# A list scheduler for the expert phase of a hybrid decoder layer on one Trainium2 core: 512-column weight pieces of half the rows, and evictions on either of two engines

## The chip, the cores and the metric

The kernel runs on 1 core of one Trainium2 chip. The metric is the device time of one execution in microseconds (us). Before the change it is 2073.69 us, the median of 3 runs (2073.25 to 2075.34).

The engines are named as in the profile: PE multiplies matrices (PEld is its loading of weights, which overlaps PE), ACT applies functions element by element, DVE combines tensors element by element, POOL issues the indirect transfers (gathers and scatters through a list of rows), and SP issues the plain transfers. Each engine works through its own queue in the order in which the program was written, and an instruction that waits holds back all that stand behind it.

## The reference, cut to what matters

The layer works on 1024 tokens of 1024 features in float32. Its first part (norm, gated linear attention and a state-space model, output projection, router) is the same in both kernels. The change lies in the second part, a mixture of experts: each token goes to 4 of 32 experts.

```
logits = xt @ router_w + router_b;  top_val, top_idx = top_k(logits, 4);  gate = softmax(top_val)
for each expert e, for the tokens that chose it (x: [n, 1024]):
    gu = x @ w_gu[e] + b_gu[e]                  # w_gu[e]: [1024, 2048]: g is the first half, up the second
    g, up = min(g, 7), clip(up, -7, 7)
    act = (up + 1) * (g * sigmoid(1.702 * g))
    y = act @ w_down[e] + b_down[e]             # w_down[e]: [1024, 1024]
    out[token] += gate * y
```

So 32 x 12 = 384 pieces of 1024 x 1024 bytes of weights are read once (402.7 MB as the profile counts).

## The kernel before, in words

**Tokens and experts.** The router writes a list of tokens for each expert, and the experts are ranked by falling count. Each rank has a fixed capacity `CAPS[r]` (396, 272, 260 ... 36; 4,648 in all; this is the column count C of its products). `GROUPS` puts the ranks into 8 groups of four with about 580 columns each, the last being ranks 3, 26, 5 and 31 (252, 68, 228, 36 columns). A group has a gate-up phase (all four experts, `w_gu`) and a down phase (all four, `w_down`).

**Weights.** A chunk is 1024 x 1024 bytes: 256 columns of all 1024 rows, so 384 chunks. SP loads it into one of 6 staging slots (`ST`, L1592). `split_chunk` makes two fp16 parts out of it, in one of 7 places (`WH`, `WL`): ACT writes the high part (L1596), and DVE, which needs ACT's result, the low part (L1597). The staging slot is free for the next load only when DVE is done.

**Products.** `products` takes one column tile of 128 at a time: for each of 8 row tiles one product of the high weights with the high tokens (L1618), one with the low tokens (L1619), one of the low weights with the high tokens (L1620). A chunk is 2 x 8 x 3 = 48 products of C columns.

**Evictions.** `run_unit` returns what is left to do with a unit's result, and the main loop puts it ahead of the next unit: ACT evicts the gate (L1661) and the up part (L1664), DVE clips and multiplies (L144, L147), ACT and DVE make the two fp16 parts (L159, L147). In the down phase ACT evicts the result (L1683) into a ring that holds 792 columns. `moe_out` then takes a block of up to 128 tokens and half of the features: 4 transposes on PE (L1697), an eviction scaled by the gate on ACT (L159, tile `A<-ax,S`) into one of 3 buffers `yt`, and a scatter with addition on POOL (L1699) into `ff_d[0]` or `ff_d[1]` in DRAM. A scatter waits for the one before it on the same half, and a `yt` buffer is free when its scatter has landed. There are 51 blocks, so 102 scatters.

**Tokens of the next group.** During a down phase POOL gathers the next group's tokens (L1602), PE transposes them (L1610, 8 for each block), and ACT (L159, tile `S<-tr`) and DVE (L147) make fp16 parts.

**What sets the order.** The order of every queue is that of the calls in the main loop. `split_to` puts splits as far ahead as the 7 places allow, `put_out` puts an output block after about 2 us of products.

## Time and profile before

| | |
|---|---|
| time, median of 3 runs | 2073.69 us |
| span of the profiled execution (first to last instruction) | 2069.1 us |
| first part, up to the first weight load of the experts | 588 us |
| expert phase, up to the last scatter's landing | about 1441 us |
| final norm and residual | about 39 us |
| PE / DVE / ACT busy, share of the span | 88% / 71% / 63% |
| moved by DMA | 540.83 MB, mean 261 GB/s |

The profiled execution's own time is shown only as its span; the median of the runs is 4.6 us more than that, which is what lies around the span. "Busy" of PE counts matmuls with modelled ends, so the idle time beside it is a lower bound. The granted clock is that of PE, 1.00 being the upper of its two levels (2.4 GHz). A DMA share over 1 means that transfers overlapped on an engine.

### The profile page before, as it was taken

The page shows a single profiled execution, that of the slowest core. Times are in us where ns is not written, and L with a number is a line of the kernel's source. Part 1 is how long each engine was busy: PE and PEld are TensorE (multiplying, and loading weights), DVE is VectorE, ACT ScalarE, POOL GpSimd, SP SyncE. Part 2 cuts the span into 40 slices and gives each one's busy share as a digit, 9 for nine tenths or more (in the row PEclk, how much of TensorE's full clock was granted, in tenths as well). Part 3 has the DMA queues.
Part 4 walks back from the last instruction along what each step waited for, and adds up shares of the span by engine and source line. Part 5 has one row for each costly group of instructions (what it writes and reads, how often), then busy time and mean ns, then how long its engine had stood idle before and what let it go on. Part 6 is the DMA issues. An engine that isn't in the chain of part 4 may idle for free. (4 is left out here: it accounts for less than half of the span.)

```text
span 2069.1 us, 53438 instructions
## 1 busy us (share of the span) xinstructions
PE 1831.0 (88%) x22354; PEld 1634.6 (79%) x22354; DVE 1465.9 (71%) x2361; ACT 1294.2 (63%) x1997; POOL 473.8 (23%) x495
## 2 busy tenths in 40 slices
PE   7678899999978999998998998999699899999950
PEld 3566788787868998997987998766599789999950
DVE  5766536567748976985894897686589668878825
ACT  3524133643326877886885887776688677888831
POOL 4720112204531033024013303201320230140033
PEclk9999899999979999999999999999899999999985
DMA  9076554323379999999999999999799999999964
GB/s 310 31 206 123 157 173 147 128 83 123 112 211 307 335 336 304 348 329 291 343 346 267 322 349 327 310 325 315 221 320 349 284 286 334 338 331 342 345 177 170
DMA packets 493413, 540.83 MB, mean 261 GB/s; under 512 B 41234, under 2 KB 459248, under 8 KB 493136
## 3 DMA queue, kind: packets, MB, share of 16 engines
q1 hardware_dynamic: 456112, 469.51, 72.4%
q0 software_dynamic: 30384, 60.49, 11.7%
q10 hardware_dynamic: 6672, 7.38, 1.1%
q8 instruction: 177, 2.90, 0.6%
q14 instruction: 68, 0.56, 0.1%
HBM read 489.57 MB, written 45.61 MB: 259 GB/s over the span
## 5 line engine op out<-in xcount | busy, mean ns | idle before, releaser
L1597 DVE SCALAR_TENSOR_TENSOR E<-A,E 128x2048 f16<-128x2048 f32 x110 | 250.5, 2289 | 92.1 <-ACT E L1596 89.4
L1699 POOL DMA_INDIRECT ff_d<-A,S x102 | 205.9, 2019 | 464.4 <-ACT A L159 252.4
L1597 DVE SCALAR_TENSOR_TENSOR B<-A,B 128x2048 f16<-128x2048 f32 x110 | 250.7, 2290 | 73.8 <-ACT B L1596 73.4
L1597 DVE SCALAR_TENSOR_TENSOR C<-A,C 128x2048 f16<-128x2048 f32 x110 | 250.5, 2289 | 52.0 <-ACT C L1596 48.8
L1620 PE MATMUL mm<-S,B 128*128 128x148 f16 (+27 forms) x1328 | 260.1, 234 | 2.9 <-DVE B L1597 2.4
L1618 PE MATMUL mm<-S,B 128*128 128x148 f16 (+27 forms) x1328 | 260.0, 234 | 2.8 <-ACT B L1596 2.1
L1618 PE MATMUL mm<-S,E 128*128 128x164 f16 (+27 forms) x1344 | 253.1, 231 | 10.2 <-ACT S L1683 10.2
L1619 PE MATMUL mm<-S,B 128*128 128x148 f16 (+27 forms) x1328 | 259.8, 233 | 0.6 <-issue 0.4
L1620 PE MATMUL mm<-S,E 128*128 128x164 f16 (+27 forms) x1344 | 253.2, 230 | 1.5 <-issue 1.5
L1619 PE MATMUL mm<-S,E 128*128 128x164 f16 (+27 forms) x1344 | 253.0, 230 | 0.9 <-issue 0.9
L1618 PE MATMUL mm<-S,C 128*128 128x92 f16 (+25 forms) x1296 | 241.2, 230 | 3.8 <-ACT S L1683 3.8
L1620 PE MATMUL mm<-S,C 128*128 128x92 f16 (+25 forms) x1296 | 241.0, 229 | 0.0
L1619 PE MATMUL mm<-S,C 128*128 128x92 f16 (+25 forms) x1296 | 240.9, 229 | 0.0
L1602 POOL DMA_INDIRECT S<-hn_d,S x51 | 80.5, 1578 | 687.6 <-PE tr L1610 647.8
L1596 ACT ACTIVATE B<-A 128x2048 f16<-128x2048 f32 x110 | 209.9, 1924 | 31.7 <-DMA A<-in_exp_w_gu_dram 27.7
L1596 ACT ACTIVATE E<-A 128x2048 f16<-128x2048 f32 x110 | 210.1, 1923 | 17.7 <-DMA A<-in_exp_w_gu_dram 9.0
L1596 ACT ACTIVATE C<-A 128x2048 f16<-128x2048 f32 x110 | 209.9, 1924 | 16.9 <-DMA A<-in_exp_w_gu_dram 9.6
L1619 PEld LDWEIGHTS <-E 128*128 128x128 f16 x1760 | 167.7, 99 | 18.8 <-issue 11.3
L1619 PEld LDWEIGHTS <-C 128*128 128x128 f16 x1760 | 171.6, 100 | 11.0 <-issue 4.3
L159 ACT ACTIVATE A<-ax,S 128x512 f32<-128x512 f32 (+17 forms) x102 | 68.5, 685 | 178.1 <-DMA ff_d<-A,S 154.2
L1618 PEld LDWEIGHTS <-B 128*128 128x128 f16 x1760 | 170.7, 99 | 10.7 <-ACT B L1596 2.4
L1619 PEld LDWEIGHTS <-B 128*128 128x128 f16 x1760 | 171.3, 100 | 9.7 <-issue 3.1
(345 smaller groups left out, 5130.0 us busy)
## 6 DMA issues: line engine op xcount, KB each, us to landing
A<-in_exp_w_gu_dram SPq DMA_DIRECT2D x256, 1024.0 KB
A<-in_exp_w_down_dram SPq DMA_DIRECT2D x128, 1024.0 KB
S<-in_ada_w_dram POOLq DMA_DIRECT2D x64, 256.0 KB, 3.1
S<-in_ada_w_dram SPq DMA_DIRECT2D x16, 512.0 KB
S<-in_w_in_dram SPq DMA_DIRECT2D x8, 1024.0 KB
S<-in_x_dram SPq DMA_DIRECT2D x12, 512.0 KB
ff_d<-S POOLq DMA_DIRECT2D x18, 256.0 KB, 6.1
S<-in_w_out_dram SPq DMA_DIRECT2D x8, 512.0 KB
```

Source lines behind the costliest of these rows:

```text
L159: A.activation(o, i, AF.Copy, scale=scale)
L1596: i_ = A.activation(wh, st, AF.Copy, scale=WS)
L1597: i_ = V.scalar_tensor_tensor(wl, st, WS, wh, op0=OP.mult, op1=OP.subtract, accum_out=acc_col())
L1602: P.indirect_dma_start(out=x_[0:cb], out_offset=None, in_=hn2_d, in_offset=bass.IndirectOffsetOnAxis(ap=x.lt[0:cb, b, 0:1], axis=0))
L1618: i_ = PE.matmul(o, wh[:, k, cols], mh[:, k], start=(k == 0), stop=False)
L1619: PE.matmul(o, wh[:, k, cols], ml[:, k], start=False, stop=False)
L1620: i_ = PE.matmul(o, wl[:, k, cols], mh[:, k], start=False, stop=(k == 7))
L1699: P.indirect_dma_start(out=ff_d[h], out_offset=bass.IndirectOffsetOnAxis(ap=lt[0:cb, b, 0:1], axis=0), in_=yt[0:cb], in_offset=None, compu ...
```

## The change

Pieces of weights are now 512 columns of half the rows (4 row tiles): still the same size and 384 of them, with rows of 2 KB in place of 1 KB. A unit (`sub_jobs`) is the gate, the up part or the result for up to 4 column tiles (2 where C is over 256). It works one piece after the other: first the 32 products with the piece's high part, then the 16 with its low part; the second piece's products add to the first's. The evictions of the up part, of its high fp16 part, of the down results, of the tokens' high part and of the output blocks may go to ACT or to DVE (`scaled`). The places for the gate are two of 1024 columns, for the up part one.

Every step is a `Job` with the engines it may run on, a duration, a due place, and the jobs it comes after. `run_jobs` walks through them at build time with a clock of its own for each engine, and at each step puts out the job that can start first (the earlier due place first on a tie); so it settles the order of all five queues and the engine of each eviction. The groups, the order of experts, the number of staging slots, of fp16 places, of `yt` buffers and of banks stay as they are. The two tables for tokens beyond the capacities (`overflow_table`) move from the fourth to the seventh unit to ahead of the first.

```diff
-    ST = [carve(t_, 0, 8, 256) for t_ in SA[:-1]]
+    ST = [carve(t_, 0, 4, 512) for t_ in SA[:-1]]
     WT.append(SA[-1])
     WH, WL = [], []
     for t_ in WT:
-        WH.append(carve(t_, 0, 8, 128).bitcast(F16))
-        WL.append(carve(t_, 4, 8, 128).bitcast(F16))
+        WH.append(carve(t_, 0, 4, 256).bitcast(F16))
+        WL.append(carve(t_, 4, 4, 256).bitcast(F16))
...
+    gs_r, u_t = [carve(e2, 0, 1024), carve(e2, 4, 1024)], carve(e3, 0, 1024)
...
-    def split_chunk(n):
-        st, wh, wl = ST[n % NST], WH[n % NWS], WL[n % NWS]
-        i_ = A.activation(wh, st, AF.Copy, scale=WS)
-        i_ = V.scalar_tensor_tensor(wl, st, WS, wh, op0=OP.mult, op1=OP.subtract, accum_out=acc_col())
...
+            x, name, col, kh = chunks[n]
+            load_expert(x)
+            SP.dma_start(ST[n % NST], I[name][0][ds(x.e, 1), 512 * kh:512 * kh + 512, col:col + 512]
+                         .rearrange("o (k p) c -> p (o k) c", p=128))
+    def split_hi(n):
+        A.activation(WH[n % NWS], ST[n % NST], AF.Copy, scale=WS)
+    def split_lo(n):
+        V.scalar_tensor_tensor(WL[n % NWS], ST[n % NST], WS, WH[n % NWS], op0=OP.mult, op1=OP.subtract,
+                               accum_out=acc_col())
...
+    def scaled(e, o, i, scale, bias=None):
+        if e == "ACT":
+            A.activation(o, i, AF.Copy if bias is None else AF.Identity, scale=scale,
+                         **({} if bias is None else {"bias": bias}))
+        elif bias is None:
+            ts(o, i, scale, OP.mult)
+        else:
+            ts(o, i, scale, OP.mult, bias, OP.add)
...
+    class Job:
+        def __init__(self, on, due, after, put, lag=0.0, behind=None):
+            self.on, self.due, self.put, self.lag = on, due, put, lag
+            self.after, self.behind = [j for j in [behind] + after if j is not None], behind
+            self.end, self.at = None, None
+            jobs.append(self)
+    def act_us(n, psum=False, parts=1):
+        return parts * (0.30 if psum else 0.22) + n / 1200
+    def dve_us(n, parts=1, rate=960):
+        return 0.13 * parts + n / rate
+    def run_jobs():
+        free = {e: 0.0 for e in ("PE", "ACT", "DVE", "POOL", "SP")}
+        users, left = {}, {}
+        for j in jobs:
+            left[id(j)] = len(j.after)
+            for a_ in j.after:
+                users.setdefault(id(a_), []).append(j)
+        open_ = [j for j in jobs if not j.after]
+        def ready(j, e):
+            return max([0.0] + [a_.end - (a_.lag if a_ is j.behind else -0.2 * (a_.at != e)) for a_ in j.after])
+        while open_:
+            best = None
+            for e in free:
+                mine = [(max(ready(j, e), free[e]), j.due, n, j) for n, j in enumerate(open_) if e in j.on]
+                if not mine:
+                    continue
+                first_ = min(m[0] for m in mine)
+                t_, due, n, j = min((m for m in mine if m[0] <= first_ + 1e-9), key=lambda m: (m[1], m[2]))
+                if best is None or (t_, due) < best[:2]:
+                    best = (t_, due, e, j)
+            t_, _, e, j = best
+            open_.remove(j)
+            j.at, free[e] = e, t_ + j.on[e]
+            j.end = free[e] + j.lag
+            j.put(e)
+            for u in users.get(id(j), ()):
+                left[id(u)] -= 1
+                if not left[id(u)]:
+                    open_.append(u)
+        assert all(j.end is not None for j in jobs)
+        return max(free.values())
...
+    subs, phase = [], []
+    for gi, g in enumerate(GROUPS):
+        phase.append((len(chunks), len(subs)))
+        for c in range(2):
+            for r in g:
+                for q, kind in enumerate("gu"):
+                    subs += [(kind, ex[r], c, js, len(chunks)) for js in (J4 if CAPS[r] <= 256 else J2)]
+                    chunks += [(ex[r], "exp_w_gu", 1024 * q + 512 * c, kh) for kh in range(2)]
+        phase.append((len(chunks), len(subs)))
+        for r in g:
+            for c in range(2):
+                subs += [("d", ex[r], c, js, len(chunks)) for js in (J4 if CAPS[r] <= 256 else J2)]
+                chunks += [(ex[r], "exp_w_down", 512 * c, kh) for kh in range(2)]
+    last_use, first_use = {}, {}
+    for i, u in enumerate(subs):
...
+        ld[n] = Job({"SP": 2.95}, n, [hi_.get(n - NST), lo_.get(n - NST)], put, lag=2.0, behind=ld.get(n - 1))
+        if n < len(chunks):
+            due = first_use[n]
+            hi_[n] = Job({"ACT": act_us(2048)}, due - 0.5, [ld[n], use.get(n - NWS), hi_.get(n - 1)], lambda e: split_hi(n))
+            lo_[n] = Job({"DVE": dve_us(2048) + 0.1}, due, [hi_[n], lo_.get(n - 1)], lambda e: split_lo(n))
...
+            t_ = Job({"PE": 0.46}, due, [gat, tr_free[q]], transpose)
+            h_ = Job({"ACT": act_us(4 * cb, True), "DVE": dve_us(4 * cb)}, due, [t_] + after[1:],
+                     lambda e, pt=pt, o_=o_: scaled(e, x.xh[o_], pt[:, :, 0:cb], XS))
+            tr_free[q] = Job({"DVE": dve_us(4 * cb) + 0.1}, due, [h_], lows)
...
+        t_ = Job({"PE": 0.46}, due, after + [ot_free[q]], transpose)
+        ot_free[q] = Job({"ACT": act_us(512, True), "DVE": dve_us(512)}, due + 2, [t_, yt_free[y]],
+                         lambda e: scaled(e, yt[0:cb], pt[0:cb].rearrange("p a b -> p (a b)"),
+                                          x.lt[0:cb, b, 1:2].bitcast(F32)))
+        yt_free[y] = added[c] = Job({"POOL": 1.7}, due, [ot_free[q], added[c]],
+                                    lambda e: P.indirect_dma_start(
+                                        out=ff_d[c], out_offset=bass.IndirectOffsetOnAxis(ap=x.lt[0:cb, b, 0:1], axis=0),
+                                        in_=yt[0:cb], in_offset=None, compute_op=OP.add), lag=7.0)
...
+        def highs(kh):
+            def put(e):
+                wh = WH[(n + kh) % NWS]
+                for q, j in enumerate(js):
+                    for k in range(4):
+                        w_, f_ = wh[:, k, 128 * j:128 * j + 128], 4 * kh + k
+                        PE.matmul(pp[q], w_, mh[:, f_], start=(f_ == 0 and q % per == 0), stop=False, skip_group_check=True)
+                        PE.matmul(pp[q], w_, ml[:, f_], start=False, stop=False, skip_group_check=True)
+            return put
+        def lows(kh):
+            def put(e):
+                wl = WL[(n + kh) % NWS]
+                for q, j in enumerate(js):
+                    for k in range(4):
+                        PE.matmul(pp[q], wl[:, k, 128 * j:128 * j + 128], mh[:, 4 * kh + k], start=False,
+                                  stop=(kh == 1 and k == 3), skip_group_check=True)
+            return put
+        for kh in range(2):
+            s_ = Job({"PE": 2 * us}, 2 * i + kh, [step[0], hi_[n + kh]] + (needs if kh == 0 else []), highs(kh))
+            step[0] = Job({"PE": us}, 2 * i + kh, [s_, lo_[n + kh]], lows(kh))
+            use[n + kh] = step[0]
+        due, end = 2 * i + 4, step[0]
...
+            ev = Job({"ACT": act_us(w, True, nj), "DVE": dve_us(w, nj)}, due, [end, u_free[0]], linear)
+            u_free[0] = Job({"DVE": dve_us(w, 2) + w / 1920}, due, [ev, gj], clamp)
+            ah = Job({"ACT": act_us(w), "DVE": dve_us(w, 1, 1920)}, due + 2, [u_free[0]],
+                     lambda e: scaled(e, x.ah[:, f0:f0 + nj], g3, XS))
+            gs_free[q] = Job({"DVE": dve_us(w)}, due + 2, [ah],
+                             lambda e: stt(x.al[:, f0:f0 + nj], g3, XS, x.ah[:, f0:f0 + nj], OP.mult, OP.subtract))
...
-    first_tokens(0)
     tables = [overflow_table(0, capr), overflow_table(1, None)]
...
+    for t_ in tables:
+        take(t_, 2)
...
+    run_jobs()
```

**DVE at the start.** The stretch begins with the copies of the transposed biases. Before (the first low part follows at once; S is the plain float32 area, tr a bank of transposes, A, B, C, E are slots of staging and fp16 parts):

```order
L1708 COPY E_4724<-tr 128x256
L142 TENSOR_SCALAR E_4724<-tr 128x256
L1708 COPY E_4724<-tr 128x256
L1597 SCALAR_TENSOR_TENSOR B_4573,A_4732<-A_4725,B_4573 128x2048
L147 SCALAR_TENSOR_TENSOR S,A_4732<-tr,S 128x4x128 x2
L147 SCALAR_TENSOR_TENSOR S,A_4732<-tr,S 128x4x76 x2
L1597 SCALAR_TENSOR_TENSOR B_4574,A_4732<-A_4726,B_4574 128x2048
```

Now, from the end of the second table on:

```order
L1498 TENSOR_REDUCE S<-S 128x1
L148 SCALAR_TENSOR_TENSOR S<-S 128x1
L1500 TENSOR_REDUCE S<-S 128x1
L133 TENSOR_TENSOR S<-S 128x1
L1507 COPY S<-tr 1x129
L1588 SCALAR_TENSOR_TENSOR B_4573,A_4732<-A_4725,B_4573 128x2048
L1588 SCALAR_TENSOR_TENSOR B_4574,A_4732<-A_4726,B_4574 128x2048
L148 SCALAR_TENSOR_TENSOR S,A_4732<-tr,S 128x4x128 x2
```

Both tables, 16 instructions and a copy each, now stand between the copies and the first low part (L1588), and two low parts stand ahead of the first tokens' low parts.

**ACT in a down phase.** This is where ranks 2 and 27 (260 and 60 columns) give their results; `A_4732<-ax,S` is the eviction of an output block into `yt`. Before:

```order
L1596 ACTIVATE C_4576<-A_4726 128x2048
L159 ACTIVATE A_4732<-ax,S 128x512 x2
L159 ACTIVATE A_4732<-ax,S 4x512
L1683 ACTIVATE S<-ax,E_4724 128x60 x2
L1596 ACTIVATE E_4577<-A_4727 128x2048
L159 ACTIVATE S<-tr 128x368 x2
L1683 ACTIVATE S<-mm,E_4724 128x60 x2
L1596 ACTIVATE E_4578<-A_4728 128x2048
```

Now:

```order
L1602 ACTIVATE A_4732<-ax,S 128x512
L1585 ACTIVATE C_4575<-A_4725 128x2048
L1602 ACTIVATE A_4732<-ax,S 4x512
L1585 ACTIVATE C_4576<-A_4726 128x2048
L1602 ACTIVATE S<-mm,E_4724 128x60 x4
L1585 ACTIVATE E_4577<-A_4727 128x2048
L1602 ACTIVATE S<-ax,E_4724 128x60 x4
L1585 ACTIVATE E_4578<-A_4728 128x2048
L1585 ACTIVATE A_4731<-A_4729 128x2048
L1585 ACTIVATE B_4573<-A_4730 128x2048
```

Three output evictions in a row became single ones with splits (L1585) between them, and the other blocks' evictions went to DVE.

**POOL at the end.** These are the scatters of the last down phase; 748 and 749 are the two halves. Before:

```order
L1699 DMA ff_d_748<-A_4732,S 1152x512 x2
L1699 DMA ff_d_749<-A_4732,S 1152x512 x2
L1699 DMA ff_d_748<-A_4732,S 1152x512
L1699 DMA ff_d_749<-A_4732,S 1152x512
L1699 DMA ff_d_748<-A_4732,S 1152x512 x2
L1699 DMA ff_d_749<-A_4732,S 1152x512 x2
L1699 DMA ff_d_748<-A_4732,S 1152x512
L1699 DMA ff_d_749<-A_4732,S 1152x512
```

Now the first five of twelve, which go on alternating to the end:

```order
L1765 DMA ff_d_748<-A_4732,S 1152x512
L1765 DMA ff_d_749<-A_4732,S 1152x512
L1765 DMA ff_d_748<-A_4732,S 1152x512
L1765 DMA ff_d_749<-A_4732,S 1152x512
L1765 DMA ff_d_748<-A_4732,S 1152x512
```

No two scatters of one half stand behind each other any more.

## Rows read from the trace of the kernel before

**Rows 1.** The page's share of busy time, its 40 slices (each of 51.7 us) for the clock, the DMA and the rate, and its two main DMA queues (packets, MB, share of 16 engines).

```profile
span 2069.1 us, 53438 instructions
PE 1831.0 (88%) x22354; PEld 1634.6 (79%) x22354; DVE 1465.9 (71%) x2361; ACT 1294.2 (63%) x1997; POOL 473.8 (23%) x495
...
DMA  9076554323379999999999999999799999999964
GB/s 310 31 206 123 157 173 147 128 83 123 112 211 307 335 336 304 348 329 291 343 346 267 322 349 327 310 325 315 221 320 349 284 286 334 338 331 342 345 177 170
...
q1 hardware_dynamic: 456112, 469.51, 72.4%
```

**Rows 2.** Busy time by stretch: the first 100 us of the expert phase's products, the stretch up to the last down phase, and what follows. Columns: the stretch, its length, busy us (and instructions) of each engine, granted clock, DMA share, GB/s.

```profile
597.00:697.00 100.00, 84.22 (x1114) 79.89 (x1114) 77.83 (x137) 65.88 (x89) 8.05 (x5) 0.88 1.04 308
597.00:1935.00 1338.00, 1251.95 (x18383) 1160.35 (x18383) 1026.18 (x1391) 1015.44 (x1431) 257.76 (x137) 0.97 1.05 318
1935.00:1997.00 62.00, 55.06 (x820) 52.15 (x817) 36.87 (x38) 39.38 (x50) 13.66 (x5) 0.99 0.95 300
```

**Rows 3.** PE's products, start us and length, with other rows between them: the first of a chunk of 116 columns, the first of the next chunk (48 products on), and two products of 36 columns that stand three apart.

```profile
802.72 0.21 PE L1618 MATMUL ax<-S,B 128*128 128x116 f16 x1
...
805.17 0.21 PE L1618 MATMUL mm<-S,C 128*128 128x116 f16 x1
...
1988.42 0.18 PE L1618 MATMUL mm<-S,C 128*128 128x36 f16 x1
...
1988.50 0.18 PE L1618 MATMUL mm<-S,C 128*128 128x36 f16 x1
```

**Rows 4.** From the chain that ended last: the transposes of a block of tokens, and of an output block (start us, us).

```profile
1779.95 0.87 PE tr L1610 x8
...
1796.92 0.45 PE ax L1697 x4
```

**Rows 5.** Waits in the stretch 600 to 1985 us: who waited for whom, us in total, times, longest us.

```profile
ACT A L159 <- DMA ff_d<-A,S: 133.0, 44, 11.8
...
DVE E L1597 <- ACT E L1596: 77.1, 37, 13.0
DVE B L1597 <- ACT B L1596: 73.4, 40, 12.8
DVE A L1597 <- ACT A L1596: 54.6, 20, 14.5
...
DVE C L1597 <- ACT C L1596: 48.8, 38, 6.3
...
PE ax L1697 <- ACT S L1683: 27.9, 14, 4.4
...
PE tr L1610 <- DMA S<-hn_d,S: 16.9, 4, 6.5
```

**Rows 6.** ACT in order of time in a down phase (start us, length, in brackets the idle time before and what ended it), and under it the busy time by stretch of the 10 us in which two of these waits lie.

```profile
1632.52 0.67 ACT L159 ACTIVATE A<-ax,S 128x512 f32<-128x512 f32 x1
1638.53 0.69 ACT L159 ACTIVATE A<-ax,S 128x512 f32<-128x512 f32 x1 [5.34 <-DMA ff_d<-A,S]
1645.08 0.68 ACT L159 ACTIVATE A<-ax,S 4x512 f32<-4x512 f32 x1 [5.86 <-DMA ff_d<-A,S]
...
1640.00:1650.00 10.00, 5.62 (x70) 5.01 (x68) 2.03 (x1) 4.92 (x9) 3.33 (x3) 0.87 0.75 226
```

**Rows 7.** Groups of instructions by line and form, 600 to 1985 us: count, busy us, mean ns of one.

```profile
L1597 DVE SCALAR_TENSOR_TENSOR C<-A,C 128x2048 f16<-128x2048 f32 x110 | 250.5, 2289 | 52.0 <-ACT C L1596 48.8 <-issue 3.1
...
L147 DVE SCALAR_TENSOR_TENSOR S<-tr,S 128x512 f16<-128x512 f32 x40 | 25.9, 685 | 0.0
...
L144 DVE TENSOR_SCALAR E<-E 128x504 f32<-128x504 f32 x4 | 1.7, 420 | 2.9 <-ACT E L1664 2.9
```

**Rows 8.** DVE and PE at the start of the expert phase, in order of time: the copies of the biases, the first product; then, from where they lie before, the first and the last of one table's 16 DVE instructions.

```profile
593.43 0.42 DVE L1708 COPY E<-tr 128x256 f32<-128x256 f32 x1 [6.07 <-PE tr L1707]
...
596.85 0.42 DVE L1708 COPY E<-tr 128x256 f32<-128x256 f32 x1 [2.66 <-PE tr L1707]
...
603.50 0.33 PE L1618 MATMUL mm<-S,B 128*128 128x204 f16 x1
...
667.56 0.18 DVE L1480 COPY S<-S 128x32 f32<-128x32 f32 x1
...
670.92 0.16 DVE L132 TENSOR_TENSOR S<-S 128x1 f32<-128x1 f32 x1
```

**Rows 9.** Busy time by stretch where rows of 4 KB (x and the weights of the modulation) are loaded, and in a dense stretch of the expert phase, where the weights come in rows of 1 KB.

```profile
25.00:30.00 5.00, 3.05 (x8) 0.41 (x7) 4.55 (x22) 2.15 (x4) 1.80 (x3) 1.00 1.02 411
680.00:740.00 60.00, 60.00 (x899) 59.82 (x898) 57.67 (x75) 51.68 (x68) 1.19 (x1) 1.00 1.10 351
```

**Rows 10.** The end, in order of time: ACT's last eviction of a gate-up phase, POOL's first and last scatter of the last down phase, SP's first load of the sums; then the row on the scatters in the view of DMA issues (count, median us from issue to landing).

```profile
1939.44 0.49 ACT L1664 ACTIVATE E<-mm,E 128x36 f32<-128x36 f32 x2
...
1958.85 1.58 POOL L1699 DMA_INDIRECT ff_d<-A,S  x1 [93.20 <-ACT A L159]
...
2023.52 1.42 POOL L1699 DMA_INDIRECT ff_d<-A,S  x1 [2.51 <-DMA ff_d<-A,S]
...
2029.72 2.33 SPq L1875 DMA_DIRECT2D S<-ff_d  x4
...
ff_d<-A,S POOLq DMA_INDIRECT x102, 7.5
```

More of the change, by code (lines that the diff above doesn't have):

```diff
@@ new lines, in hybrid_layer_kernel @@
+    y0_free = [j for l_ in x_ready.values() for j in l_]
+    for i, u in enumerate(subs):
+        while made < min(len(chunks) + 5, u[4] + 2):
+            chunk_jobs(made)
+            made += 1
+        if i_ph % 2 and i_ph < len(phase) - 1 and phase[i_ph][1] == i:
+            todo = [(ex[r], b) for r in GROUPS[i_ph // 2 + 1] for b in range(NBS[r])]
+            span_ = 2 * (phase[i_ph + 1][1] - i)
+            for k, (x, b) in enumerate(todo):
+                token_jobs(x, b, 2 * i + (span_ - 4) * k / len(todo), [ld[phase[i_ph - 1][0]], step[0]])
+        if i_ph < len(phase) and phase[i_ph][1] <= i:
+            i_ph += 1
+        sub_jobs(i, *u)
```

304 lines of the change are left out of this document (130 added, 174 removed).

## The prediction

> **What bounds the kernel now.** I read the page's slices first: after the first slice the DMA moves 31 to 211 GB/s up to the twelfth, and from there 221 to 349, but for the last two, with its engines at nine tenths or more in nearly every slice [rows 1]. That is the expert phase, the only part that the diff touches. Then the busy time by stretch: from 597 us, where PE transposes the first tokens, to 1935 us PE is busy for 1251.95 of 1338 us, DVE for 1026, ACT for 1015, and the DMA share is 1.05 at 318 GB/s [rows 2]. PE and DMA are both near their limit and neither is at it.
>
> So how much must PE do? 48 products of 116 columns take 805.17 - 802.72 = 2.45 us, 51.0 ns each, which is 116/2.4 + 2.7 ns; three of 36 columns take 0.08 us, so about 25 ns is the least [rows 3]. An expert takes 24 column tiles x 8 row tiles x 3 = 576 products. For 4,648 columns: 576 x 4648/2400 = 1115.5 us, 576 x 32 x 2.7 ns = 50 us, and 9 us for the three ranks below 54 columns: 1174 us. Transposes: 51 blocks at 0.87 us in, 102 at 0.45 us out [rows 4]: 44 + 46. Together 1264 us. The last down phase is a third of its group's 150 us and 12 output blocks, 55 us, so 1209 us lie before it. It begins at about 1939 us, with the last gate-up eviction [rows 10]: 1342 us after 597. **133 us are lost**, against 86 us of idle time and a granted clock of 0.97 (3% of 1338 is 40 us) by the stretch [rows 2], which add up to nearly that.
>
> Where? In the first 100 us 16 us idle and a clock of 0.88 [rows 2]: 28 us. The other 105 us lie mostly in down phases. There the longest waits say what happens: ACT waits 133 us in all for scatters to leave a `yt` buffer, and DVE waits 77 + 73 + 55 + 49 = 254 us for the high part of a chunk from ACT [rows 5]. The order of time shows the two joined: ACT stands 5.34 and 5.86 us ahead of output evictions, no split is made meanwhile, and in the 10 us from 1640 PE is busy for 5.62 us, DVE for 2.03, and even the DMA falls to 226 GB/s, as staging slots are not freed [rows 6]. An eviction that needs nothing but time holds back the weights of the next product.
>
> At the end the order is another: the last down phase's twelve scatters start at 1958.85 and the sums are loaded at 2029.72 [rows 10], 91 us after the phase began, whereas its PE work is 55 us. That chain of scatters, not PE, sets the end.
>
> **The change part by part.** *Work of PE:* the same 384 x 48 products and the same transposes, 1209 us before the last down phase. That high and low products stand apart changes only that the low part may come later: 32 of 48 products go ahead without it, which takes a part of DVE's lag off PE's path.
>
> *Load of ACT and DVE:* counted in the built order, DVE gets 94 evictions without a bias (433 columns on average), 104 with one (139 columns) and 49 conversions of activations (570 columns). The trace has 0.42 us for 256 columns out of PSUM [rows 8], 0.69 for 512 [rows 7], so about 0.15 us + columns/960: 56 + 31 us; and 0.42 us for 504 columns inside SBUF [rows 7]: 22 us. Against that wider units save 141 longer and 70 shorter instructions at about 0.12 us: 26 us. Net +83 us. DVE goes from 1026 + 37 = 1063 us [rows 2] to about 1145, ACT falls by about 130 to 925. In the dense stretch DVE is busy for 57.67 of 60 us [rows 9], so 1145 us fit under PE's 1264 at 91%. I cost this at nothing: PE's work covers it. If the cover is gone, the net 83 us are the price (below).
>
> *Rows of 2 KB:* the packets of the weights' queue are 469.51 MB/456112 = 1029 bytes [rows 1], and with them a dense stretch gives 351 GB/s; rows of 4 KB gave 411 [rows 9]. A straight line through the time of a packet on 16 engines (46.7 and 159 ns) gives 84 ns for 2 KB, 389 GB/s: an estimate, with 351 and 411 as its ends. The phase moves 402.7 MB of weights and 2 x 4648 x 4 KB = 38 MB of gathers and scatters. At 351 GB/s that is 1256 us, 1844 us if it began at 588; at 389 it is 1133 us. Either is under PE's work, so the rate has no term of its own; it lets the staging slots fill again sooner after a gap. The Trainium skill ("DMA: Bandwidth & Descriptors", Specifications) gives 512 B as the least transfer for line rate, so rows of 1 KB would be at it already and 2 KB would win nothing. The 351 and 411 GB/s speak against it. By the rule the rate stays, which is the third rival below (2057 us); by the rows it rises, and the sum stands as it is.
>
> *Start:* both tables now stand on DVE ahead of the first low part. One table is 667.56 to 671.08, 3.5 us, and needs PE and a copy behind (about 1 us). The bias copies end at 597.3 [rows 8]; two tables bring DVE to about 606, two low parts and two tokens' low parts (2.29 and 0.69 us [rows 7]) to 612, two more pairs to 618. The first product stood at 603.5 and will stand near 618. In exchange six pieces are staged and split by then, so the ramp that follows, with its low clock, is shorter. I take 25 us lost in the start in place of 28.
>
> *Down phases:* the jobs give a scatter 1.7 us and 7 us of lag; the trace has a median of 7.5 us from issue to landing [rows 10]. So most output evictions will stand in the queues where their buffer is free already, with splits between them, and half of them on DVE. What goes is the head-of-line waiting, the bulk of the 105 us. What may stay are waits of PE for output transposes behind ACT (27.9 us) and for gathered tokens (16.9) [rows 5]. Bounds: 0 (no gap left) and 105 (all stays). I take 38, nearer to the low end, as those two rows less some of the first come to that.
>
> *End:* the first output transposes stand behind rank 3's two halves (192 products of 252 columns, 20.7 us) and one half of rank 26 (3 us), so the first scatter comes about 25 us into the phase, not 20. Alternating halves no longer wait for their own predecessor at once. Six pairs, one every 7.5 + 0.3 us, the second of a pair 1.9 us behind: 25 + 39 + 1.9 + 7.5 = 73.4, say 74 us in place of 91. After the loads 2069.1 - 2029.7 = 39.4 us remain, unchanged.
>
> *Sum:* 597 + 25 + 1209 + 38 + 74 + 39.4 = 1982.4 us of span, against 2069.1 of the profiled execution. The median of the runs is 4.6 us above that span, so I forecast **1987 us**, 4.2% less.
>
> **The rivals.** *The scatters still pace the down phases.* For it: three `yt` buffers, two transposing banks and the chain on each half are as before; single scatters took up to 11.8 us of a wait [rows 5], more than the jobs allow, and now DVE, fuller, can be the engine that is held. Against it: a down phase has 12 to 14 scatters, 175 us to the next one, and the result ring holds two thirds of a group. All 105 us stay: 2054 us.
>
> *No gap is left.* For it: all four engines have spare time on average. Against it: the order is fixed at build time and groups mix 252 with 36 columns, with 7 places for parts. 1987 - 38 = 1949 us.
>
> *The transfers are the pacemaker, and the change doesn't do what it says there.* If the average rate stays at 318 GB/s [rows 2] with 2 KB rows, the last down phase begins where it did, and only the end's 17 us are won: about 2057 us. Against it: DMA falls where slots are not freed [rows 6], so the average is a result, not a cause.
>
> *Slower: DVE becomes the bound.* From 597 to 1997 us DVE is idle for 337 us and busy for 1063 [rows 2]; 254 us of the idle time are waits for ACT's high parts [rows 5]. If the static order keeps DVE behind ACT as now, each evicted column on DVE lengthens the phase: 2073.7 + 83 = about 2157 us. It decides from the point where less than 83 of the 337 idle us go; for my forecast some 170 must go.
>
> **How the numbers follow.** The likeliest case, 1955 to 2030 us, gets 0.54; no gap left 0.13; scatters still pacing 0.16; transfers 0.06; DVE 0.11. 0.2% of the time, 4 us, is about what a measurement of this kernel tells from no change. Faster: 0.54 + 0.13 + 0.16 + 0.05; a little of the last two cases falls on no change, 0.03, and the rest, 0.09, on slower. The range leaves out the DVE case and the lowest tail: 1940 to 2060 us.
>
> **What would show it.** In the profile after: ACT's wait for scatters far under 133 us; DVE's waits for high parts far under 254 us, with DVE above 80% of the phase; PE idle for 30 to 45 us between the first product and the last down phase, at a clock of 0.98 or more; the first product near 618 us; the sums' load some 74 us after the last gate-up eviction; dense stretches over 351 GB/s. Wrong would be: PE waiting for DVE's low parts (then DVE is the bound), output evictions that wait for scatters on DVE as they did on ACT, or gaps of PE in gate-up phases, which I have costed at nothing.

## The result, and the profile after

The changed kernel takes 2025.28 us (median of 4 runs, 2024.69 to 2031.31) against 2073.47 for the kernel before beside it: a ratio of 0.9768, 95% interval 0.9754 to 0.9783. That is 48 us less. The forecast was 1987 us, within 1940 to 2060: the direction and the range held, the value was 38 us too low.

The page of the changed kernel: span, busy time, scatters, the weights' queue.

```profile
span 2022.9 us, 53263 instructions
PE 1806.0 (89%) x22354; PEld 1614.5 (80%) x22354; DVE 1544.2 (76%) x2396; ACT 1199.1 (59%) x1682; POOL 526.5 (26%) x495
...
q1 hardware_dynamic: 259504, 469.51, 67.5%
...
L1765 POOL DMA_INDIRECT ff_d<-A,S x102 | 260.7, 2555 | 353.8 <-DVE A L143 141.2
```

Busy time by stretch, same columns as [rows 2]: the first 100 us, from there to the last gate-up eviction, from the first product to that eviction, the tail up to the load of the sums, and the dense stretch of [rows 9].

```profile
597.00:697.00 100.00, 85.68 (x1221) 82.70 (x1222) 85.92 (x127) 69.68 (x81) 21.10 (x7) 0.89 1.03 344
597.00:1902.00 1305.00, 1233.01 (x18449) 1147.79 (x18450) 1103.63 (x1407) 930.30 (x1137) 312.13 (x139) 0.97 0.98 330
614.00:1902.00 1288.00, 1227.41 (x18419) 1143.75 (x18418) 1088.21 (x1370) 920.84 (x1129) 300.39 (x136) 0.98 0.98 329
1902.00:1984.00 82.00, 59.30 (x813) 54.39 (x811) 36.70 (x48) 35.73 (x45) 24.23 (x12) 0.83 0.66 189
680.00:740.00 60.00, 60.00 (x911) 59.76 (x909) 58.06 (x70) 45.94 (x59) 2.39 (x3) 1.00 1.00 358
```

Waits in 600 to 1985 us (who for whom, us in total, times, longest); they answer to [rows 5]. `L1602` and `L143` with the tile `A` are the evictions of output blocks into a `yt` buffer, on ACT and on DVE; `L1588` is the low split, `L1585` the high one, `L1759` the transposes of output blocks.

```profile
POOL ff_d L1765 <- DVE A L143: 141.2, 12, 103.6
ACT A L1602 <- DMA ff_d<-A,S: 103.9, 24, 13.0
...
DVE A L143 <- DMA ff_d<-A,S: 31.0, 10, 8.1
...
PE ax L1759 <- ACT A L1602: 22.4, 6, 12.4
...
DVE B L1588 <- ACT B L1585: 21.0, 10, 5.2
...
PE ax L1759 <- DVE A L143: 18.5, 7, 6.1
...
DVE E L1588 <- ACT E L1585: 15.8, 11, 6.6
```

Three things stand out. DVE's waits for high parts fell from 254 us to 48, as forecast. The evictions' waits for scatters did not fall: 133 us before, 103.9 + 31.0 = 135 us now. And a scatter's issue on POOL, 2.02 us in the mean in the kernel before (this row of its page), now takes 2.56:

```profile
L1699 POOL DMA_INDIRECT ff_d<-A,S x102 | 205.9, 2019 | 464.4 <-ACT A L159 252.4
```

POOL, DVE and ACT in order of time, in one of the down phases, show the longest such issue:

```profile
1790.77 15.05 POOL L1765 DMA_INDIRECT ff_d<-A,S  x1 [3.44 <-DVE B L1588]
1806.12 1.57 POOL L1765 DMA_INDIRECT ff_d<-A,S  x1 [0.30 <-issue]
```

```profile
1790.37 0.74 DVE L143 TENSOR_SCALAR A<-ax,S 64x512 f32<-64x512 f32 x1
1791.03 2.27 DVE L1588 SCALAR_TENSOR_TENSOR C<-A,C 128x2048 f16<-128x2048 f32 x1
...
1793.24 2.27 DVE L1588 SCALAR_TENSOR_TENSOR C<-A,C 128x2048 f16<-128x2048 f32 x1
...
1795.45 2.28 DVE L1588 SCALAR_TENSOR_TENSOR E<-A,E 128x2048 f16<-128x2048 f32 x1
...
1797.66 2.28 DVE L1588 SCALAR_TENSOR_TENSOR E<-A,E 128x2048 f16<-128x2048 f32 x1
...
1799.88 2.28 DVE L1588 SCALAR_TENSOR_TENSOR A<-A,A 128x2048 f16<-128x2048 f32 x1
...
1802.09 2.28 DVE L1588 SCALAR_TENSOR_TENSOR B<-A,B 128x2048 f16<-128x2048 f32 x1
1804.30 0.07 DVE L1588 DVE_READ_ACCUMULATOR B<-A,B 128x1 f32 x1
```

```profile
1812.39 0.68 ACT L1602 ACTIVATE A<-ax,S 64x512 f32<-64x512 f32 x1 [13.04 <-DMA ff_d<-A,S]
```

The scatter is begun while DVE works through six low splits without a pause, and it is done 1.5 us after the last. The next one, with DVE at rest, takes 1.57 us. ACT's next output eviction stands 13.04 us for a scatter to land, the longest of all these waits. In the kernel before, DVE rested 254 us in waits between splits, and no issue in 600 to 1985 us took over 4.05 us.

The tail: ACT's last eviction of a gate-up phase, the first and the last scatter, the load of the sums [rows 10].

```profile
1900.92 0.84 ACT L1602 ACTIVATE E<-mm,E 128x36 f32<-128x36 f32 x4 [4.33 <-issue]
```

```profile
1928.79 3.36 POOL L1765 DMA_INDIRECT ff_d<-A,S  x1 [103.57 <-DVE A L143]
...
1977.43 1.40 POOL L1765 DMA_INDIRECT ff_d<-A,S  x1 [1.29 <-DMA ff_d<-A,S]
```

```profile
1983.66 2.14 SPq L1980 DMA_DIRECT2D S<-ff_d  x4
```

### The profile page after: what moved, and what is told of

Its sections match the earlier page's. It is cut to its first block, busy times and chain, and to the rows that moved or that the text cites. A ratio compares the mean times of both kernels' runs of the same rounds, so it can differ in the third digit from the quotient of the medians.

```text
span 2022.9 us, 53263 instructions
## 1 busy us (share of the span) xinstructions
PE 1806.0 (89%) x22354; PEld 1614.5 (80%) x22354; DVE 1544.2 (76%) x2396; ACT 1199.1 (59%) x1682; POOL 526.5 (26%) x495
## 5 line engine op out<-in xcount | busy, mean ns | idle before, releaser
L1765 POOL DMA_INDIRECT ff_d<-A,S x102 | 260.7, 2555 | 353.8 <-DVE A L143 141.2
L1588 DVE SCALAR_TENSOR_TENSOR B<-A,B 128x2048 f16<-128x2048 f32 x110 | 249.5, 2285 | 33.1 <-ACT B L1585 21.0
L1588 DVE SCALAR_TENSOR_TENSOR E<-A,E 128x2048 f16<-128x2048 f32 x110 | 249.7, 2285 | 16.0 <-ACT E L1585 15.8
L1588 DVE SCALAR_TENSOR_TENSOR C<-A,C 128x2048 f16<-128x2048 f32 x110 | 249.7, 2284 | 8.3 <-ACT C L1585 8.2
L1585 ACT ACTIVATE B<-A 128x2048 f16<-128x2048 f32 x110 | 209.2, 1917 | 46.7 <-DMA A<-in_exp_w_gu_dram 36.7
L1585 ACT ACTIVATE E<-A 128x2048 f16<-128x2048 f32 x110 | 208.9, 1917 | 33.1 <-DMA A<-in_exp_w_gu_dram 18.4
L1585 ACT ACTIVATE C<-A 128x2048 f16<-128x2048 f32 x110 | 208.7, 1920 | 25.9 <-PE ax L1792 15.3
L1791 PE MATMUL mm<-S,E 128*128 128x92 f16 (+29 forms) x1336 | 187.8, 230 | 0.6 <-issue 0.5
L1791 PE MATMUL mm<-S,B 128*128 128x164 f16 (+28 forms) x1364 | 185.3, 227 | 3.3 <-issue 3.2
L1792 PE MATMUL mm<-S,B 128*128 128x164 f16 (+28 forms) x1364 | 184.9, 227 | 3.8 <-issue 3.8
L1792 PE MATMUL mm<-S,E 128*128 128x92 f16 (+29 forms) x1336 | 187.5, 229 | 0.0
L1792 PE MATMUL mm<-S,C 128*128 128x92 f16 (+28 forms) x1352 | 183.0, 226 | 3.2 <-issue 3.0
L1791 PE MATMUL mm<-S,C 128*128 128x92 f16 (+28 forms) x1352 | 183.2, 227 | 1.7 <-ACT S L1602 1.7
L1791 PEld LDWEIGHTS <-B 128*128 128x128 f16 x1760 | 154.3, 98 | 16.8 <-issue 9.4
L1791 PEld LDWEIGHTS <-C 128*128 128x128 f16 x1760 | 153.3, 98 | 13.0 <-issue 6.3
L1791 PEld LDWEIGHTS <-E 128*128 128x128 f16 x1760 | 155.0, 98 | 9.6 <-issue 2.0
L1792 PEld LDWEIGHTS <-B 128*128 128x128 f16 x1760 | 154.2, 98 | 9.4 <-issue 2.1
L1792 PEld LDWEIGHTS <-E 128*128 128x128 f16 x1760 | 154.9, 98 | 7.9 <-issue 0.4
L1792 PEld LDWEIGHTS <-C 128*128 128x128 f16 x1760 | 153.0, 98 | 8.3 <-issue 1.8
L148 DVE SCALAR_TENSOR_TENSOR S<-S 128x1 f32<-128x1 f32 (+7 forms) x249 | 106.0, 434 | 42.2 <-DMA S<-in_ada_w_dram 28.4
L1588 DVE SCALAR_TENSOR_TENSOR A<-A,A 128x2048 f16<-128x2048 f32 x54 | 123.5, 2286 | 3.1 <-ACT A L1585 2.9
```

The source lines that it names most:

```text
L148: V.scalar_tensor_tensor(o, a, s, b, op0=op0, op1=op1, **kw)
L1585: A.activation(WH[n % NWS], ST[n % NST], AF.Copy, scale=WS)
L1588: V.scalar_tensor_tensor(WL[n % NWS], ST[n % NST], WS, WH[n % NWS], op0=OP.mult, op1=OP.subtract, accum_out=acc_col())
L1765: lambda e: P.indirect_dma_start(out=ff_d[c], out_offset=bass.IndirectOffsetOnAxis(ap=x.lt[0:cb, b, 0:1], axis=0), in_=yt[0:cb], in_offset ...
L1791: PE.matmul(pp[q], w_, mh[:, f_], start=(f_ == 0 and q % per == 0), stop=False, skip_group_check=True)
L1792: PE.matmul(pp[q], w_, ml[:, f_], start=False, stop=False, skip_group_check=True)
```

## The experiments

Each is an edit of the changed kernel. A ratio is to the kernel before on the same chip; 0.001 is 2.1 us, and the changed kernel has 0.9768. The first question was whether the missing gain lies in the waits for scatters, in a DVE that is full, or at the start.

**Six buffers for output blocks.**

```
-    yt_r = [carve(a7, 2 * i, 512) for i in range(3)]
+    yt_r = [carve(a7, 2 * i, 512) for i in range(3)] + [view(kb, 512) for kb in (60.875, 64, 66)]
```

> The changed kernel (2025.3 us) with six buffers for evicted output blocks instead of three; nothing else. Theory 1 (the forecast's gap term was too small because output evictions wait in the order of their engine for a buffer whose scatter has not landed: 104 us of such waits on ACT, 31 on DVE): the waits for ff_d on ACT and DVE fall from 135 us to under 40, the transposes of output blocks on PE no longer wait 38 us for those evictions, and the time falls by 20 to 35 us, to 1990 to 2005. Rival (the scatters are a chain of their own: each waits for the last one into the same half of the result, so more buffers only let the evictions run ahead and POOL waits instead): the waits move to POOL, the time falls by less than 10 us. Rival (DVE, 99 per cent busy in stretches of the gate-up phases, sets the pace): within 5 us of 2025.

Measured: 0.9588 [0.9552, 0.9624], 37 us under the changed kernel. The evictions' waits for scatters fell from 135 to 44 us, both a little outside what I expected. Here are all four rows of them (`S` is the tile of the new buffers):

```profile
DVE A L143 <- DMA ff_d<-A,S: 19.7, 2, 14.8
...
ACT S L1602 <- DMA ff_d<-S: 13.3, 4, 5.0
...
ACT A L1602 <- DMA ff_d<-A,S: 6.7, 1, 6.7
...
DVE S L143 <- DMA ff_d<-S: 4.4, 1, 4.4
```

PE's waits for output evictions in front of their transposes fell from 41 to 14 us; 10.8 of the 14 stand behind the one wait of 14.8 us on DVE. Theory 1 holds. The rival on the chain of scatters was right in one point: POOL's own waits for the scatter before on the same half grew from 86 to 135 us, first the row of the changed kernel, then the two of this one:

```profile
POOL ff_d L1765 <- DMA ff_d<-A,S: 86.0, 23, 8.5
```

```profile
POOL ff_d L1765 <- DMA ff_d<-A,S: 78.2, 23, 11.0
...
POOL ff_d L1765 <- DMA ff_d<-S: 57.2, 13, 7.9
```

But the time fell by 37 us and not by less than 10, so those waits are not what sets it, and neither is a full DVE. The planner knows of the six buffers, so the order of the queues differs too.

**A dearer scatter in the plan.**

```
-        yt_free[y] = added[c] = Job({"POOL": 1.7}, due, [ot_free[q], added[c]],
+        yt_free[y] = added[c] = Job({"POOL": 2.5}, due, [ot_free[q], added[c]],
...
-                                        in_=yt[0:cb], in_offset=None, compute_op=OP.add), lag=7.0)
+                                        in_=yt[0:cb], in_offset=None, compute_op=OP.add), lag=9.5)
```

> The changed kernel with the plan's price of a scatter raised from 1.7 us on POOL and 7.0 us to landing to 2.5 and 9.5; the program's work is the same, the planner alone orders it otherwise. Theory 1: the planner puts the evictions that wait for a buffer later in their engine's row, so that the waits for ff_d on ACT and DVE fall by a third or more from 135 us, and the time falls by 5 to 25 us. Rival (DVE sets the pace, or the scatter chain does): within 5 us of 2025, or slower, since a planner with dearer scatters can only delay what hangs on them.

Measured: 0.9627 [0.9602, 0.9652], 29 us less where I expected 5 to 25, and the waits are down to 27 us:

```profile
ACT A L1602 <- DMA ff_d<-A,S: 23.6, 12, 3.8
...
DVE A L143 <- DMA ff_d<-A,S: 3.2, 3, 1.7
```

Nothing but two numbers of the plan differs, so it is the order, an eviction put where its buffer is not yet free, that cost it. The other order also shortens a scatter's issue, from 2.56 to 2.25 us in the mean; how much of the 29 us comes by that is not shown.

**Both together.** The two edits above in one kernel.

> Six buffers for output blocks and the dearer scatter in the plan together. The runs before gave 0.9588 for the first and 0.9627 for the second alone, against 0.9768 for the changed kernel. If both take away the same waits (evictions held for a buffer whose scatter has not landed), the sum is little more than the better of them: 0.952 to 0.959. If they work on different waits (the buffers on the evictions, the plan on POOL's chain of scatters and the gathers behind it), 0.945 to 0.952.

Measured: 0.9603 [0.9584, 0.9622], just above the first of the two ranges: no better than the buffers alone. They take away the same waits.

**High and low products mixed again.** One job waits for both parts.

```
-            s_ = Job({"PE": 2 * us}, 2 * i + kh, [step[0], hi_[n + kh]] + (needs if kh == 0 else []), highs(kh))
-            step[0] = Job({"PE": us}, 2 * i + kh, [s_, lo_[n + kh]], lows(kh))
+            step[0] = Job({"PE": 3 * us}, 2 * i + kh, [step[0], hi_[n + kh], lo_[n + kh]] + (needs if kh == 0 else []),
+                          products(kh))
```

> The changed kernel with the three products of a piece put out again in one job, by block of 128 rows, which waits for the high and the low part of the piece, instead of all high products ahead of all low ones. By the prediction's reading (PE now works on high products while DVE makes the low part, about 3.0 us of low split on DVE beside 2 x 0.82 us of high products for a pair of column blocks): with pieces loaded and split ahead by up to as many buffers as there are, this order matters little where the splits run ahead, and costs up to 2 us at a piece where DVE is late; 10 to 40 us slower than 2025. Rival (the splits always run far enough ahead; the gain comes from the order of evictions and the two engines alone): within 5 us of 2025.

Measured: 0.9787 [0.9765, 0.9808], which overlaps the changed kernel's interval. My expectation missed and the rival held: the splits run far enough ahead, and the order of products is worth at most a few us. (A low split takes 2.28 us, as the rows above show, and not the 3.0 of the expectation.)

**Rows of 1 KB again, and the same count of transfers with rows of 2 KB.** The first kernel loads a piece as two transfers of 256 columns, the second as two transfers of half the rows.

```
+            for q in range(2):
+                SP.dma_start(ST[n % NST][:, :, 256 * q:256 * q + 256],
+                             I[name][0][ds(x.e, 1), 512 * kh:512 * kh + 512, col + 256 * q:col + 256 * q + 256]
...
+            for q in range(2):
+                SP.dma_start(ST[n % NST][:, 2 * q:2 * q + 2],
+                             I[name][0][ds(x.e, 1), 512 * kh + 256 * q:512 * kh + 256 * q + 256, col:col + 512]
```

> The changed kernel with each weight piece loaded by two transfers of 256 columns (rows of 1 KB, as before the change) instead of one of 512 (rows of 2 KB); the bytes, the pieces and all other work are the same. Theory (PE is busy 95 per cent of the expert phase, and the transfers have slack: 331 GB/s in the phase against 358 in a dense stretch): the DMA share of the dense stretch 680 to 740 rises, and the time moves by less than 10 us. Rival (transfers set the pace, and the longer rows are where the gain comes from): 30 us slower or more, with waits of the split for the pieces' transfers, which are now close to none.

> The changed kernel with each piece loaded by two transfers of half its rows each: as many transfers (757 of 512 KB) as in the run with rows of 1 KB, but rows of 2 KB as in the changed kernel. The run with rows of 1 KB gave 0.9900 against 0.9768, with 344 GB/s in the dense stretch 680 to 740 and a DMA share of 1.08, against 358 and 1.00. If the length of the rows made that, this one stands at 0.975 to 0.981, with a DMA share near 1.00 and 355 GB/s or more; if the number of transfers did (SP's issues, the queue's places), at 0.987 to 0.993, with 350 GB/s or less.

Measured: 0.9900 [0.9880, 0.9921] with rows of 1 KB, 27 us over the changed kernel, and 0.9800 [0.9775, 0.9825] with two half transfers. The first missed my expectation of under 10 us and came close to the rival's 30; the second fell into the case for the length of the rows. The dense stretch, and the weights' queue over the whole span, first with rows of 1 KB, then with two halves:

```profile
680.00:740.00 60.00, 60.00 (x912) 59.76 (x910) 58.06 (x70) 47.95 (x61) 2.99 (x3) 1.00 1.08 344
```

```profile
q1 hardware_dynamic: 462256, 469.53, 72.0%
```

```profile
680.00:740.00 60.00, 60.00 (x900) 59.76 (x898) 57.75 (x69) 45.95 (x56) 1.86 (x2) 1.00 1.02 360
```

```profile
q1 hardware_dynamic: 265648, 469.53, 67.9%
```

By these shares the same bytes keep the 16 engines busy for 1483 us of the span of 2060.4 in rows of 1 KB, and for 1381 us of 2034.6 in rows of 2 KB. ACT's waits for weights in front of high splits are 169 us with rows of 1 KB, 60 in the changed kernel and 76 with two halves; the largest row of the first, and the same in the changed kernel:

```profile
ACT E L1587 <- DMA A<-in_exp_w_gu_dram: 53.9, 32, 9.3
```

```profile
ACT E L1585 <- DMA A<-in_exp_w_gu_dram: 18.4, 14, 4.7
```

So the length of the rows makes some 20 of the 27 us; the rest, 7 us, may be the number of transfers, but the intervals of the changed kernel and of two halves overlap, so that is not shown. The Trainium skill ("DMA: Bandwidth & Descriptors", Specifications) puts the least transfer for line rate at 512 B. By that the first kernel would stand where the second does, and it does not (0.9900 against 0.9800).

**Rows of 1 KB with six buffers.** The two edits in one kernel.

> Six buffers for output blocks, and the pieces loaded by two transfers of 256 columns each (rows of 1 KB). The changed kernel with rows of 1 KB alone came to 0.9900 against 0.9768. If the transfers then set the pace (the splits waited over 100 us for pieces), the six buffers give nothing back: 0.985 to 0.992. If the shorter rows hurt only by making the scatters land later, and the evictions wait for those, six buffers give back most of it: 0.962 to 0.970. Between them, both count.

Measured: 0.9805 [0.9784, 0.9825], between the two cases. Against six buffers alone the shorter rows cost 45 us, more than the 27 beside three buffers, and ACT waits 261 us for weights: with the evictions' waits gone the transfers are next in line.

**The overflow tables after the expert phase.**

```
-    for t_ in tables:
-        take(t_, 2)
...
     run_jobs()
+    for t_ in tables:
+        take(t_, 2)
```

> Six buffers for output blocks, and the two overflow tables worked out after the expert phase instead of ahead of it; nothing else against six buffers alone (0.9588). In the changed kernel the tables take the engines until 602 us and the first product is at 613.7, before the change at 603.5. Theory (the start is on the path: PE waits for the first token blocks, which the tables hold up): the first product comes 6 to 12 us earlier and the time falls by 4 to 10 us, to 0.954 to 0.957, less what the tables cost at the end, some 5 us where nothing else runs. Rival (the tables' work is only moved, from a place where the first weights are awaited anyway to the end, where all is on the path): no change or up to 10 us slower, 0.959 to 0.964.

Measured: 0.9631 [0.9596, 0.9667] against 0.9588 [0.9552, 0.9624]: no gain. The start is not where the missing time is.

**All scaling evictions on ACT.** The choice of engine is taken back at each of the five places, as here:

```
-        ot_free[q] = Job({"ACT": act_us(512, True), "DVE": dve_us(512)}, due + 2, [t_, yt_free[y]],
+        ot_free[q] = Job({"ACT": act_us(512, True)}, due + 2, [t_, yt_free[y]],
```

> The changed kernel with every eviction that only scales (token blocks, linear halves, activations' high parts, results, output blocks) given to ACT alone, as before the change; the planner, the pieces and the rows stay as changed. Theory (the load of DVE is what the change moves: 44 output blocks, the biases' products and others go from ACT to DVE, and DVE is busy 1099 of 1298 us, ACT 928; with them back, ACT stands near 1000 and DVE near 1020): output evictions queue on ACT alone behind splits and scatters, as in the kernel before; the time rises by 10 to 30 us above the 0.977 of the changed kernel, to 0.98 to 0.99 of the kernel before. Rival (the gain comes from the rows and the pieces; the two engines only share a load that is hidden): within 5 us of the changed kernel, 0.975 to 0.979.

Measured: 0.9670 [0.9628, 0.9712], 20 us *faster* than the changed kernel: both of my cases missed, and beside three buffers this part of the change costs time. The plan, and with it the order of the queues, differs too. The waits of DVE are back (232 us for high parts), those for scatters fell to 75, and a scatter's issue takes 2.08 us, none over 3.74:

```profile
L1765 POOL DMA_INDIRECT ff_d<-A,S x102 | 212.5, 2083 | 378.5 <-ACT A L1602 265.4 <-DMA ff_d<-A,S 77.9 <-issue 20.6
```

That gave a new theory: it is DVE's pauses that let POOL write a scatter.

**A low split that reads one input.**

```
-        V.scalar_tensor_tensor(WL[n % NWS], ST[n % NST], WS, WH[n % NWS], op0=OP.mult, op1=OP.subtract,
-                               accum_out=acc_col())
+        V.tensor_scalar(WL[n % NWS], ST[n % NST], WS, 0.0, op0=OP.mult, op1=OP.add, accum_out=acc_col())
```

The jobs and their prices are untouched, so every queue has the order of the changed kernel.

> The changed kernel with DVE's low split made from the loaded piece alone (scale and accumulate, one input from SBUF) instead of from the piece and its high part (two inputs); the low part is then not the remainder, so the values of the result are off, but every product, eviction and transfer is there. It also drops DVE's wait for the high part (48 us in all), so DVE has if anything fewer pauses. Seen so far: POOL's issue of a scatter takes 2.56 us in the mean in the changed kernel, up to 15.05 us, and the long ones end when DVE's row of low splits ends (issue 1790.77 to 1805.82, DVE busy without a pause 1787.5 to 1804.4); in the kernel before it took 2.02, at most 4.05, and with all scalings on ACT, where DVE pauses 220 us for high parts, 2.08, at most 3.74. Theory (the two-input split on DVE keeps POOL from writing the scatter's descriptors, so a DVE without pauses makes the scatters late, and the evictions wait for them): the mean issue falls under 2.1 us, none is over 4.5 us, and the time falls to 0.960 to 0.970 of the kernel before. Rival (the issue is long because POOL or the transfers are loaded, whatever DVE reads): the mean stays at 2.4 to 2.6 us with issues over 5 us, and the time within 5 us of the changed kernel.

Measured: 0.9675 [0.9628, 0.9721], 19 us less, and all three numbers lie where the theory put them. Groups of 600 to 1985 us, a split and the scatters:

```profile
L1588 DVE TENSOR_SCALAR_CACHE_REDUCE C<-A 128x2048 f16<-128x2048 f32 x110 | 249.0, 2279 | 4.9 <-PE mm L1799 4.1 <-DMA A<-in_exp_w_gu_dram 0.4 <-PE mm L1791 0.4
...
L1764 POOL DMA_INDIRECT ff_d<-A,S x102 | 162.9, 1597 | 419.6 <-DVE A L143 170.4 <-DMA ff_d<-A,S 107.6 <-ACT A L1601 74.7
```

The split takes as long as before (2279 against 2284 ns) and DVE rests less between splits, yet a scatter's issue falls from 2555 to 1597 ns, the longest from 15.05 to 2.45 us, and the evictions' waits for scatters from 135 to 73 us. What DVE reads, not how busy it is, lengthens the issue. The Trainium skill ("SBUF — State Buffer", Who interferes with whom) says that a DVE instruction with two SBUF inputs contends with a GpSimd instruction that reads SBUF, and that one with a single input outside the two-port modes does not. Both runs agree, with 2555 and 1597 ns, if the issue of a scatter, which takes its list of rows from the tile `x.lt`, counts as such an instruction. The edit also drops DVE's 48 us of waits for high parts, and the first product comes 5 us sooner (608.81 against 613.73), so how much of the 19 us is the issue alone stays open; that the kernel with 232 us of such waits is just as fast speaks for the issue.

**All on ACT with six buffers, and with rows of 1 KB.**

> Six buffers for output blocks, and every scaling eviction on ACT alone. Alone they gave 0.9588 and 0.9670 against 0.9768. If all on ACT is faster because the scatters are issued sooner (2.08 against 2.56 us, so the evictions wait less), both take away the same waits and the sum is no better than six buffers alone: 0.955 to 0.962. If it is faster because DVE was full in the gate-up phases, the two add up: 0.945 to 0.953.

> Every scaling eviction on ACT alone, and the pieces loaded in two transfers of 256 columns (rows of 1 KB): of the change, the order of pieces with half the rows and high products first, and a planner over all engines, are left. Rows of 1 KB cost 27 us in the changed kernel and 45 us with six buffers, evictions on ACT alone gained 20. If the rows cost as much here as transfers that set the pace do: 0.983 to 0.992, close to the kernel before; if the rows hurt only through full DVE and late scatters: 0.970 to 0.975.

Measured: 0.9589 [0.9536, 0.9642], the same as six buffers alone, so evictions on ACT and more buffers take away the same waits, and a full DVE is not a bound behind them. With rows of 1 KB and all on ACT: 0.9804 [0.9757, 0.9852], between its two cases. This kernel keeps of the change the pieces of half the rows with their wider units, the order of products, the early tables and the planner, and the steps along this one path are: 1 to 0.9804 for these (41 us less), to 0.9670 with rows of 2 KB (28 less), to 0.9768 with evictions on either engine (20 more). Its pieces come in two transfers each, those of the kernel before in one, so a part of the second step, up to the 7 us seen above, may belong to the first.

The fastest are the kernels with six buffers, 0.9588 and 0.9589; the second had a median of 1987.41 us.

## Why the prediction was right, and where it was not

*The work of PE and the start held, the end nearly.* First product at 613.73 us (forecast 618). The first 100 us lose 14 us to idle time and 11 to the clock of 0.89, together 25, as forecast. The end, from the last gate-up eviction at 1902 us to the load of the sums at 1984, is 82 us against 74 forecast and 91 before: the first scatter came 27 us into it (25 forecast), but from the first to the last it took 48.6 us against 41, and the first two issues took 3.36 us each. What remains after the load is 39 us, as before. The 4.6 us that I added for what lies around the span were too many: the median of the runs is 2.4 us above the span of 2022.9.

*The gap term failed: 38 us forecast, 71 measured.* Lost before the last down phase are 1902 - 597 - 1209 = 96 us, less the 25 of the start. (Idle time and clock of the stretch give 111 in place of 96: 72 us, and 3% of 1305.) With the 8 us of the tail this is the whole distance: 33 + 8 = 41, where the span is 40.5 us above the sum. I had left only waits for output transposes and for gathered tokens in this term, because the plan's 1.7 and 7 us for a scatter stood beside a median of 7.5, and so counted on the waits for scatters to go. Two things were wrong with that. A buffer is waited for when its scatter is late, so the late landings count and not the median. POOL and ACT in a down phase:

```profile
1608.65 2.10 POOL L1765 DMA_INDIRECT ff_d<-A,S  x1 [0.30 <-issue]
...
1622.94 1.48 POOL L1765 DMA_INDIRECT ff_d<-A,S  x1 [9.61 <-ACT A L1602]
```

```profile
1622.15 0.68 ACT L1602 ACTIVATE A<-ax,S 4x512 f32<-4x512 f32 x1 [8.16 <-DMA ff_d<-A,S]
```

```profile
1622.88 1.06 PE L1759 MATMUL ax<-S 128*60 128x128 f32 x4 [12.40 <-ACT A L1602]
```

The eviction waits for a scatter to land, and no scatter was issued after 1608.65: 13.5 us at least from issue to landing. PE's output transposes wait 12.40 us for that eviction, the longest such wait of PE. And the scatters became later through the change itself. What I named as a sign of being wrong, "output evictions that wait for scatters on DVE as they did on ACT", is in the trace: 31 us on DVE beside 104 on ACT.

*By what way a held eviction reaches PE was read wrong.* The prediction says that it holds back the weights of the next product. But PE waited only 4.5 us for parts of weights in the kernel before, by these two rows of 600 to 1985 us:

```profile
PE mm L1620 <- DVE B L1597: 2.4, 2, 2.0
...
PE mm L1618 <- ACT B L1596: 2.1, 1, 2.1
```

Its long waits are those of [rows 5], in front of output transposes (27.9 us) and for gathered tokens (16.9), and in the changed kernel 34 of its 61 idle us before the last down phase are waits of output transposes for evictions. This fits that the order of high and low products, which I took to relieve PE, gives nothing that was measured.

*DVE's load was sized right and its cost was not nothing.* DVE is busy for 1104 us up to 1902 (85%, forecast over 80%), and for 1140 with the end, where 1145 were forecast. PE waits for low parts 5 us in all; the rival in which DVE is the bound fell with the run that has six buffers and all on ACT. But the cover I named was PE's work, and the price came by another way: a DVE that goes from one two-input split to the next keeps POOL from issuing scatters. All on ACT gains 20 us; that is the price of the choice of engine beside three buffers, and with six buffers there is none (0.9588 and 0.9589).

*Rows of 2 KB had no term and are worth 20 to 28 us in the changed kernel.* The rate of the dense stretch rose in the direction the rows said (358 GB/s, short of the estimate of 389). But that rate is no limit of the rows: with all evictions on ACT, rows of 2 KB move only 344 there, at a lower DMA share:

```profile
680.00:740.00 60.00, 60.00 (x935) 59.76 (x933) 50.84 (x61) 49.01 (x65) 3.98 (x3) 1.00 0.97 344
```

I reasoned from an average that stays under PE's work. The splits' waits for weights, 169 us with rows of 1 KB and 60 without, show that transfers are late in places all the same. In the kernel before, with rows of 1 KB, those waits were 54 us; no run put longer rows into it, so what they would be worth there alone is not shown. The gain of 48 us is thus made of other parts than those forecast, and the rival on transfers described a mechanism that does count.

*Of the signs:* PE is idle for 61 us between the first product and the last down phase (30 to 45 forecast) at a clock of 0.98 (as forecast). With the waits for scatters mostly gone, as I had assumed, the chip gives 0.9588, about 1988 us, close to the forecast. The parts come near it too: with six buffers the last gate-up eviction ends at 1877 us and the sums are loaded at 1956, so 1877 - 597 - 1209 - 26 = 45 us are lost where 38 were forecast, and the end takes 80 us. So it was read right that evictions waiting for scatters are what opens the gaps; the planned lag did not remove them.

## What to carry to other kernels

A list scheduler is as good as its longest latencies: plan a transfer that frees a buffer by its late cases, or give it more buffers, since an eviction that waits in an in-order queue holds back all behind it. Before work is moved onto an engine that rests, ask what its rests are used for: here POOL issued its scatters in them. And a resource whose average is below the bound can still be worth a term; the waits at its consumers say how much.

## What the runs showed of the hardware that was not expected

A scatter's issue on POOL took 1.60 us in the mean and 2.45 at most beside one-input splits on DVE. Beside two-input splits of the same length it took 2.56 in the mean, and an unbroken chain of six, each 2.28 us, held one for 15.05 us. With as many transfers of the same bytes, rows of 1 KB kept the DMA engines busy for 1483 us and rows of 2 KB for 1381; in the dense stretch they moved 344 and 360 GB/s at DMA shares of 1.08 and 1.02, and the kernel's time differed by 20 us.
